# Low parts of ff1 weight chunks made by an accumulating DMA instead of a vector subtraction, and one low part of the first activations issued earlier

## The chip, the core and the metric

The kernel runs on one core of a Trainium2 chip. Its engines are TensorE (PE, with its weight loads PEld), VectorE (DVE), ScalarE (ACT), GpSimd (POOL) and SyncE (SP), which work side by side and wait for one another by semaphores. Sixteen DMA engines move data between HBM and the on-chip memory SBUF. The metric is the device time of one execution in microseconds (us); lower is better.

## The reference

One decoder layer over 256 positions of width 1024: two attention mixers side by side, their merge, and then the feed-forward part, which is all that the change touches. In the reference it is

```
h2 = rmsnorm(x, norm2_g[layer])
u = jax.nn.relu(h2 @ w_ff1[layer])          # w_ff1: 1024 x 4096
x = x + (u * u) @ w_ff2[layer]              # w_ff2: 4096 x 1024
return rmsnorm(x, norm_f_g)
```

Everything is float32.

## The kernel before

**Split products.** TensorE multiplies in a rounded format (float32r). To keep float32 accuracy each operand is split into a high part (the value rounded) and a low part (what the rounding left out), and each product is three matmuls: high times high, high times low, low times high (`mm3`, line 219). So every weight that is loaded must be split before use: `split` (line 103) lets ScalarE write the high part `whi` (line 112, a copy that rounds) and VectorE the low part `wlo = raw - whi` (line 114).

**Chunks and slots.** The weights come in chunks of 128 x 2048 float32 (1 MB), listed in `CHUNKS` (line 23) and loaded from HBM by SP's queue (`load`, line 98) into three rotating buffers `raw`. `whi` and `wlo` have three rotating buffers each too. The kernel's loop handles one chunk per slot: slot c runs the matmuls of chunk c. The feed-forward part starts at c = 28 (`C_FF`): chunk 28 is ff1 number 0, then ff1 and ff2 chunks alternate: odd c from 29 to 49 are ff1 numbers 1 to 11, even c from 30 to 50 are ff2 numbers 0 to 10. From 51 to 54 come ff1 12 to 15, from 55 to 59 ff2 11 to 15.

**An ff1 slot** is 48 matmuls of 256 columns (`wstat`, lines 239 to 247). Of each three, in the order in which the trace shows them, the third is the one that reads `wlo`. **An ff2 slot** of numbers 0 to 10 uses a scheme of seven products instead of eight (`seven_mms`, line 869): 21 matmuls of 512 columns. It needs sums of the chunk's blocks (`w_sums`, lines 838 to 845, VectorE), a split of the sums (`w_parts`, lines 855 to 862: ScalarE, then VectorE), and a split of the single blocks (`w_singles`, lines 847 to 853: ScalarE `sh`, VectorE `sl`). It also needs the activations of the ff1 slot two slots earlier: `squares` (lines 802 to 805, ScalarE), `act_sums` (line 813, VectorE) and `act_parts` (lines 820 and 822: ScalarE `ah`, VectorE `al`).

**The order.** Each engine executes its instructions in the order in which the program issues them. That order is written by hand: `at(pos, f, ...)` puts a call at the fraction pos of a slot's matmuls, and `run_slot` (line 202) issues the calls between the matmuls, sorted by position; calls of one position stand in the order in which they were put. `slot_events(c)` (line 920) prepares chunk c + 2 (and c + 3 for ff2), and issues the load of chunk c + 5, which must wait until the `raw` buffer of chunk c + 2 has had its last reader. `squares_events(i)` (line 947) is run in the slot behind ff1 number i. In slot 29 there are also the transposes of the residual into four output banks (`x1_rows`, line 754, copied out by ScalarE at line 761), the same banks in which slot 30 starts its products. In slot 32, `rstd2` (line 825) puts two squares on ScalarE.

Of the kernel before, what the change touches and what calls it, by code (L numbers as in the profile page):

```python
# [9 lines left out]
F32R = mybir.dt.float32r  # L10
AF = mybir.ActivationFunctionType
ALU = mybir.AluOpType
# [10 lines left out]
CHUNKS = (  # L23
    [("kva", i, 1536) for i in range(2)]
    + [("kvb", i, 1632) for i in range(2)]
    + [(s, i, 2048) for s in ("q", "qm", "km", "vm") for i in range(2)]
    + [("gm", i, 2048) for i in range(8)]
    + [("upn", i, 2048) for i in range(2)]
    + [("upm", i, 2048) for i in range(2)]
    + [("wout", i, 2048) for i in range(4)]  # L30
    + [("ff1", 0, 2048)]
# [4 lines left out]
NCH = len(CHUNKS)  # L36
# [9 lines left out]
def hybrid_layer(ctx: ExitStack, tc: tile.TileContext, gxd, w, w1c, small, const, gf, out):  # L46
    nc = tc.nc
    act, dve, pool, pe = nc.scalar, nc.vector, nc.gpsimd, nc.tensor
    PS = bass.MemoryType.PSUM

    wp = ctx.enter_context(tc.tile_pool(name="wp", bufs=3))
# [36 lines left out]
    raw, hi, lo = {}, {}, {}  # L88
# [110 lines left out]
    def at(pos, f, *a):  # L199
        ev.append((pos, f, a))  # L200
# [333 lines left out]
    for sec, c0, n in groups:  # L534
# [6 lines left out]
        for i in range(2):  # L541
            c = c0 + i
# [86 lines left out]
    for g in range(4):  # L629
        accs = [acc_tile(), acc_tile()]  # L630
        for i in range(2):
            c = C_GM + 2 * g + i
# [40 lines left out]
    for sec, c0, kind, evac in (("upn", C_UPN, "n", upn_evac), ("upm", C_UPM, "m", upm_evac)):  # L673
        for i in range(2):
            c = c0 + i
# [26 lines left out]
    def two_blocks(c, ah, al, late=8, whole=None):  # L702

        if late < 8:
            outs = [acc_tile()[:, 0:256] for _ in range(2)]
            whole = None
            order = [range(late), range(late, 8)]
        else:
            whole = whole or acc_tile()
            outs = [whole[:, 0:256], whole[:, 256:512]]  # L710
            order = [range(8)]
        mms = []
        for ks in order:
            for m in range(2):
                mms += wstat(outs[m], c, m * 128, 8, 256, ah, al, ks=ks, last=7)
        return mms, outs, whole
# [46 lines left out]
    for i in range(4):  # L763
        c = C_WOUT + i
# [20 lines left out]
        else:  # L785
            mms, outs, _ = two_blocks(c, mxh, mxl, 4 if i == 0 else 8)
# [48 lines left out]
    def seven(c):  # L835
        return c < NCH and CHUNKS[c][0] == "ff2" and CHUNKS[c][1] < NSEVEN
# [71 lines left out]
    def ff2_mms(i, c, p):  # L908
# [8 lines left out]
                     k == 1 and i == (13 if p == order[3] else 15))  # L917
        return r

    def slot_events(c):  # L920

        ff1 = CHUNKS[c][0] == "ff1"
        for d in (2, 3):
            if seven(c + d):
                first = c + d == C_FF + 2
                if d == 3 and not first:
                    at(0.5, w_singles, c + d, "h")
                    at(0.55, w_sums, c + d)
                elif d == 2 and first:
                    at(0.3, w_singles, c + d, "h")  # L930
                    at(0.5, w_sums, c + d)
                    at(0.55, w_parts, c + d, "h")
                    at(0.6, w_singles, c + d, "l")
                    at(0.75, w_parts, c + d, "l")
                    at(0.8, load, c + 5)
                elif d == 2:
                    at(0.05, w_singles, c + d, "l")
                    at(0.3, w_parts, c + d, "h")
                    at(0.5, w_parts, c + d, "l")
                    at(0.55, load, c + 5)  # L940
        if c + 2 < NCH and not seven(c + 2):
            for k in range(2):
                at(0.3 * k, split, c + 2, k, 2, "h")
            at(0.46, split, c + 2, 0, 1, "l")
            at(0.51, load, c + 5)

    def squares_events(i, outs, whole):
        at(0.02, squares, i, outs, whole)
        at(0.25, act_sums, i)
        at(0.4, act_parts, i, "h")  # L950
        at(0.6, act_parts, i, "l")

    fst, x1, scr = None, None, None
    for c in range(C_FF, NCH - 2):
        sec, i, _ = CHUNKS[c]
        if c == C_FF:
            lo_late(0.03, c - 1)
        slot_events(c)
        for f, a in prev:
            if f is wout_evac:  # L960
# [4 lines left out]
        if sec == "ff1":  # L965
# [13 lines left out]
            if i == NSEVEN + 1:  # L979
                at(0.1, combine, 0)  # L980
                at(0.35, combine, 1)
                at(0.7, combine, 2)
            run_slot(mms)
            prev = [(squares_events, (i, outs, whole))]
        elif i < NSEVEN:
            if i == 0:
# [147 lines left out]
```

## Time and profile before

| | |
|---|---|
| median of 3 runs | 391.09 us (390.72 to 391.92) |
| the profiled execution: its own time | 391.41 us |
| the profiled execution: span of the trace | 389.5 us |
| feed-forward slots 28 to 59 | from about 200 us to the end |

How to read what follows: the page of the profile gives for each engine its busy time, and a map of the span in 40 slices of about 9.7 us, each digit the busy share in tenths. "PEclk" is the clock that TensorE was granted, in tenths of full speed. A timeline row has the start, the duration, the engine, the line of the kernel, the instruction, what it writes and reads, and how many were merged into the row; in brackets stands idle time just before it and who ended it. A matmul's duration includes its passage through the array, so rows of back-to-back matmuls overlap: the distance from start to start is what one costs.

### The profile page before, as it was taken

What the parts mean: (1) busy time and instruction counts of PE and PEld (TensorE: products, weight loads), DVE (VectorE), ACT (ScalarE), POOL (GpSimd) and SP (SyncE); (2) the same over time, 40 slices, a digit from 0 to 9 for tenths busy, and PEclk for the clock granted to TensorE, in tenths of its full rate; (3) what the DMA queues carried; (4) which work ended last, traced back from release to release, by engine and by line L of the source; (5) the groups of instructions that cost most, each with busy time, mean ns of one, the idle gap of its engine ahead of it and who ended that gap; (6) DMA issues with size and microseconds to landing.
All of it is one profiled execution on the core that took longest, in us unless ns stands there. A gap on an engine that the chain in (4) does not pass through costs nothing.

```text
span 389.5 us, 5979 instructions
## 1 busy us (share of the span) xinstructions
PE 373.1 (96%) x2407; PEld 324.4 (83%) x2407; DVE 305.5 (78%) x443; ACT 231.4 (59%) x368; POOL 3.8 (1%) x14
## 2 busy tenths in 40 slices
PE   7999999999999999999998799999999999889993
PEld 6997888878888788779998599999998888888783
DVE  4968677887876869666969968999999999922565
ACT  6884455766755747444457567776666668451712
POOL 1000000000000000000000000000000000000001
PEclk9999999999999999999999699999999999999998
DMA  7977435233533334530846633566655556554003
GB/s 248 406 264 270 165 106 203 108 115 118 202 109 109 134 151 151 213 108 18 316 155 218 215 108 121 204 217 215 217 193 186 174 207 217 213 178 146 0 2 109
DMA packets 11260, 66.31 MB, mean 170 GB/s; under 512 B 1248, under 2 KB 2784, under 8 KB 3936
## 3 DMA queue, kind: packets, MB, share of 16 engines
q1 hardware_dynamic: 10800, 65.14, 46.8%
q10 hardware_dynamic: 432, 0.79, 0.5%
q8 instruction: 19, 0.31, 0.3%
q14 instruction: 9, 0.07, 0.0%
HBM read 64.87 MB, written 1.05 MB: 169 GB/s over the span
## 4 chain that ended last, share of the span: by engine, by line
PE 82%; DVE 8%; ACT 4%; issue 2%; DMA 1%; SPq 1%; POOLq 0%; POOL 0%; DVEq 0%; ACTq 0%
PE acc L217 51%; PE o L217 11%; PE yb L217 5%; PE tp L217 4%; DVE wlo L114 3%; PE kvbacc L217 2%; ACT whi L112 2%; PE qacc L217 2%; PE Sa L217 1%; DMA raw<-in_kva_dram 1%; PE Sb L217 1%; PE Sa L482 1%; PE Sb L482 1%; PE tp L298 1%; DVE wlo L862 1%
## 5 line engine op out<-in xcount | busy, mean ns | idle before, releaser
L114 DVE TENSOR_TENSOR wlo<-raw,whi 128x1024 fp32r<-128x1024 f32 (+3 forms) x87 | 114.5, 1333 | 28.9 <-ACT whi L112 28.8
L112 ACT ACTIVATE whi<-raw 128x1024 fp32r<-128x1024 f32 (+2 forms) x106 | 99.7, 975 | 46.9 <-PE acc L217 33.3
L217 PE MATMUL acc<-h2h,whi 128*128 128x256 f32 x240 | 66.8, 278 | 3.0 <-ACT ur L804 3.0
L217 PE MATMUL acc<-h2h,wlo 128*128 128x256 f32 x240 | 66.5, 277 | 0.0
L217 PE MATMUL acc<-h2l,whi 128*128 128x256 f32 x240 | 66.5, 277 | 0.0
L217 PE MATMUL acc<-whi,hTh 128*128 128x512 f32 (+1 forms) x128 | 50.8, 397 | 0.8 <-ACT whi L112 0.6
L217 PE MATMUL acc<-wlo,hTh 128*128 128x512 f32 (+1 forms) x128 | 50.6, 395 | 0.4 <-DVE wlo L114 0.2
L217 PE MATMUL acc<-whi,hTl 128*128 128x512 f32 (+1 forms) x128 | 49.4, 386 | 0.0
L217 PEld LDWEIGHTS acc<-h2h,whi 128*128 128x128 f32 x240 | 45.1, 188 | 3.9 <-ACT ur L804 3.4
L217 PEld LDWEIGHTS acc<-h2l,whi 128*128 128x128 f32 x240 | 45.1, 188 | 0.5
L217 PEld LDWEIGHTS acc<-h2h,wlo 128*128 128x128 f32 x240 | 45.1, 188 | 0.0
L860 ACT ACTIVATE whi<-wt 128x2048 fp32r<-128x2048 f32 x11 | 21.1, 1920 | 24.7 <-DVE wt L845 24.7
L217 PEld LDWEIGHTS acc<-whi,hTh 128*128 128x128 f32 x128 | 24.2, 189 | 6.8 <-ACT whi L112 1.1
L217 PEld LDWEIGHTS acc<-wlo,hTh 128*128 128x128 f32 x128 | 24.1, 188 | 5.5 <-DVE wlo L114 1.6
L217 PEld LDWEIGHTS acc<-whi,hTl 128*128 128x128 f32 x128 | 24.1, 188 | 4.3
L862 DVE TENSOR_TENSOR wlo<-wt,whi 128x2048 fp32r<-128x2048 f32 x11 | 25.1, 2286 | 0.4 <-ACT whi L860 0.4
L820 ACT ACTIVATE ah<-aq 128x896 fp32r<-128x896 f32 (+1 forms) x16 | 13.6, 852 | 18.1 <-PE o L217 10.0
L822 DVE TENSOR_TENSOR al<-aq,ah 128x896 fp32r<-128x896 f32 (+1 forms) x16 | 15.4, 960 | 6.7 <-ACT ah L820 6.7
L853 DVE TENSOR_TENSOR sl<-raw,sh 128x1536 fp32r<-128x1536 f32 x11 | 19.3, 1752 | 0.0
L217 PE MATMUL o<-wlo,ah 128*128 128x512 f32 (+1 forms) x47 | 18.9, 402 | 0.0
L217 PE MATMUL o<-whi,al 128*128 128x512 f32 (+1 forms) x47 | 18.8, 400 | 0.0
L217 PE MATMUL o<-whi,ah 128*128 128x512 f32 (+1 forms) x47 | 18.8, 400 | 0.0
(280 smaller groups left out, 759.5 us busy)
## 6 DMA issues: line engine op xcount, KB each, us to landing
raw<-in_ff_dram SPq DMA_DIRECT2D x32, 1024.0 KB, 4.8
raw<-in_gm_dram SPq DMA_DIRECT2D x8, 1024.0 KB, 4.8
raw<-in_wout_dram SPq DMA_DIRECT2D x4, 1024.0 KB, 4.8
raw<-in_q_dram SPq DMA_DIRECT2D x2, 1024.0 KB, 5.5
raw<-in_qm_dram SPq DMA_DIRECT2D x2, 1024.0 KB, 7.6
raw<-in_km_dram SPq DMA_DIRECT2D x2, 1024.0 KB, 5.8
raw<-in_vm_dram SPq DMA_DIRECT2D x2, 1024.0 KB, 4.8
raw<-in_upn_dram SPq DMA_DIRECT2D x2, 1024.0 KB, 4.8
```

The source lines that it names most:

```text
L112: act.activation(hi[c][:, a:b], raw[c][:, a:b], AF.Copy)
L114: dve.tensor_tensor(lo[c][:, a:b], raw[c][:, a:b], hi[c][:, a:b].bitcast(F32), op=ALU.subtract)
L217: pe.matmul(o, l, r, start=start, stop=stop, skip_group_check=True)
L298: pe.transpose(tp[:, j * 256 + t * 128:j * 256 + t * 128 + 128], src[:, t, (2 * i + j) * 128:(2 * i + j + 1) * 128], ident)
L482: pe.transpose(S[x][:, j, c:c + 128], P[:, 2 * x + j, c:c + 128], ident)
L820: act.activation(A[i][1][:, 0:b - a], aq[:, a:b], AF.Copy)
L822: dve.tensor_tensor(A[i][2][:, 0:b - a], aq[:, a:b], A[i][1][:, 0:b - a].bitcast(F32), op=ALU.subtract)
L853: dve.tensor_tensor(singles[c][1], v, singles[c][0].bitcast(F32), op=ALU.subtract)
L860: act.activation(hi[c], v, AF.Copy)
L862: dve.tensor_tensor(lo[c], v, hi[c].bitcast(F32), op=ALU.subtract)
```

## The change

Two edits. First, a new function `lo_by_dma` makes the low part of some ff1 chunks. ScalarE writes `lo = -raw`, rounded to float32r, which is the negated high part; then a DMA issued from POOL's queue reads the same chunk's raw weights from HBM once more and adds them onto `lo` in SBUF, so that `lo` becomes raw minus rounded raw. The high part is then written by one ScalarE copy of 128 x 2048 in place of two of 128 x 1024, and VectorE's subtraction of line 114 is not issued for these chunks. This holds in the slots c where chunk c + 1 is an ff2 chunk of the seven-product kind and chunk c + 2 is not: c = 29, 31, ..., 49, so for the chunks 31, 33, ..., 51 (ff1 numbers 2 to 12, eleven by this condition). `lo_by_dma` stands at the start of slot c, the high part at 0.3, the next load at 0.51. Second, for ff1 number 0 alone `act_parts(0, "l")` stands at 0.42 of slot 29 instead of 0.6.

```
+    def lo_by_dma(c):
+
+        sec, j, _ = CHUNKS[c]
+        hi[c] = wp.tile([128, 2048], F32R, name="whi")
+        lo[c] = wp.tile([128, 2048], F32R, name="wlo")
+        act.activation(lo[c], raw[c], AF.Copy, scale=-1.0)
+        pool.dma_start(out=lo[c], in_=w[sec][j], accum_op=ALU.add)
+
...
-        if c + 2 < NCH and not seven(c + 2):
+        if c + 2 < NCH and not seven(c + 2) and seven(c + 1):
+            at(0.0, lo_by_dma, c + 2)
+            at(0.3, split, c + 2, 0, 1, "h")
+            at(0.51, load, c + 5)
+        elif c + 2 < NCH and not seven(c + 2):
             for k in range(2):
                 at(0.3 * k, split, c + 2, k, 2, "h")
             at(0.46, split, c + 2, 0, 1, "l")
...
         at(0.4, act_parts, i, "h")
-        at(0.6, act_parts, i, "l")
+        at(0.6 if i else 0.42, act_parts, i, "l")
```

## The prediction

> **What bounds the kernel now.** I read the map of slices first. TensorE stands at nine tenths nearly everywhere, so it is the bound on the whole; the exceptions matter.
>
> ```profile
> span 389.5 us, 5979 instructions
> PE   7999999999999999999998799999999999889993
> DVE  4968677887876869666969968999999999922565
> PEclk9999999999999999999999699999999999999998
> ```
>
> Two things stand out. In slices 22 and 23 (214 to 234 us, the first feed-forward slots) TensorE drops to 8 and 7 and its clock to 6. And from slice 25 to 34 (244 to 341 us) VectorE too is at nine. Which of the two binds there I read from the chain of work that ended last, which shows where each ff1 slot (48 matmuls) starts:
>
> ```profile
> 224.83 5.45 PE acc L217 x48
> ...
> 286.79 5.47 PE acc L217 x48
> ...
> 329.19 5.37 PE acc L217 x47
> ```
>
> 224.83 is slot 31, 286.79 slot 43, 329.19 slot 51. Six pairs of slots (one ff1, one ff2) take 61.96 us, 10.33 each; the last four take 42.40, 10.60 each. VectorE's work in this stretch, grouped by shape:
>
> ```profile
> L114 DVE TENSOR_TENSOR wlo<-raw,whi 128x2048 fp32r<-128x2048 f32 x11 | 25.2, 2287 | 5.8 <-ACT whi L112 5.8
> L862 DVE TENSOR_TENSOR wlo<-wt,whi 128x2048 fp32r<-128x2048 f32 x9 | 20.6, 2285 | 0.0
> ...
> 260.80 2.29 DVE L114 TENSOR_TENSOR wlo<-raw,whi 128x2048 fp32r<-128x2048 f32 x1
> ...
> 271.40 2.28 DVE L114 TENSOR_TENSOR wlo<-raw,whi 128x2048 fp32r<-128x2048 f32 x1
> ```
>
> The last two rows, from VectorE's timeline, are the same subtraction in two neighbouring pairs: 10.60 apart. So VectorE needs 10.60 us per pair without a pause, TensorE 10.33. VectorE falls 0.27 behind per pair from the moment it has no pause, eats up its lead in six pairs, and is the bound in the last four.
>
> **The start** I read from the waits of TensorE and the rows of slots 29 and 30:
>
> ```profile
> PE o L217 <- DVE al L822: 2.2, 1, 2.2
> PE o L217 <- ACT x L761: 1.9, 1, 1.9
> ...
> 206.46 1.92 ACT L860 ACTIVATE whi<-wt 128x2048 fp32r<-128x2048 f32 x1 [4.12 <-DVE wt L845]
> 208.28 1.04 ACT L112 ACTIVATE whi<-raw 128x1024 fp32r<-128x1024 f32 x1
> 209.23 0.64 ACT L802 ACTIVATE ur<-acc 128x256 f32<-128x256 f32 x2
> 209.90 0.64 ACT L805 ACTIVATE aq<-ur 128x512 f32<-128x512 f32 x1
> 210.44 1.05 ACT L112 ACTIVATE whi<-raw 128x1024 fp32r<-128x1024 f32 x1
> 211.74 0.95 ACT L820 ACTIVATE ah<-aq 128x896 fp32r<-128x896 f32 x1 [0.26 <-DVE aq L813]
> 212.60 1.47 ACT L851 ACTIVATE sh<-raw 128x1536 fp32r<-128x1536 f32 x1
> 213.97 2.04 ACT L761 ACTIVATE x<-o 128x512 f32<-128x512 f32 x4
> ...
> 211.56 2.28 DVE L114 TENSOR_TENSOR wlo<-raw,whi 128x2048 fp32r<-128x2048 f32 x1
> ...
> 216.35 1.08 DVE L822 TENSOR_TENSOR al<-aq,ah 128x896 fp32r<-128x896 f32 x1
> ...
> 212.42 0.28 PE L217 MATMUL acc<-h2h,wlo 128*128 128x256 f32 x1
> 214.60 0.50 PE L217 MATMUL o<-sh,ah 128*128 128x512 f32 x1 [1.90 <-ACT x L761]
> 214.93 0.40 PE L217 MATMUL o<-sl,ah 128*128 128x512 f32 x1
> 217.49 0.79 PE L217 MATMUL o<-sh,al 128*128 128x512 f32 x1 [2.16 <-DVE al L822]
> ```
>
> Slot 29 ends at 212.7. Slot 30 waits first for ScalarE to empty its output bank, runs two matmuls, and then waits for `al`, which on VectorE stands behind the subtraction for chunk 31 and the sums for chunk 32, although its input `ah` was ready at 212.69. TensorE idles about 4.1 us, and pays again, for the clock falls:
>
> ```profile
> 216.00:217.00 1.00, 0.00 (x0) 0.00 (x0) 1.00 (x2) 0.97 (x3) 0.00 (x0) 0.77 0.89 352
> ...
> 223.00:224.00 1.00, 1.00 (x5) 0.77 (x5) 0.24 (x1) 0.00 (x0) 0.00 (x0) 0.82 0.24 98
> ```
>
> In these windows the third number from the end is the granted clock: 0.77 of a microsecond that mixes full and half speed puts the fall at 216.5, 0.82 puts the return at 223.4. From 217.49 to 223.4 TensorE works 5.9 us at half speed, which loses 2.95.
>
> **The change, part by part.** *Pairs.* VectorE loses one row of 2.287 us per pair: 10.60 - 2.29 = 8.31, below TensorE's 10.33. The four slow pairs become TensorE-bound: 4 x 0.27 = **1.1 us gained**. ScalarE must now carry it:
>
> ```profile
> L860 ACT ACTIVATE whi<-wt 128x2048 fp32r<-128x2048 f32 x9 | 17.3, 1923 | 20.6 <-DVE wt L845 20.6
> L851 ACT ACTIVATE sh<-raw 128x1536 fp32r<-128x1536 f32 x9 | 13.2, 1472 | 0.0
> L820 ACT ACTIVATE ah<-aq 128x896 fp32r<-128x896 f32 x9 | 8.6, 957 | 6.7 <-DVE aq L813 6.7
> L805 ACT ACTIVATE aq<-ur 128x512 f32<-128x512 f32 x10 | 6.3, 633 | 0.3
> L804 ACT ACTIVATE ur<-acc 128x512 f32<-128x512 f32 x10 | 5.8, 577 | 2.1 <-PE acc L217 2.1
> ```
>
> Per pair: three 128x2048 copies (negated low, high, sums) at 1.92, and 1.47, 0.96, 0.63, 0.58: 9.4 us of 10.33. In order from a pair's start: the two new copies and `sh` end near 5.2, before the accumulator that `ur` waits for is complete (5.47); `ur`, `aq`, `whi`, `ah` end near 9.6. It fits, with 0.7 to spare, so I cost it at nothing; were each copy 0.25 longer, it would bind.
>
> *The accumulating DMA* is what the trace does not show. It can start only when ScalarE has written `-raw` into a `wlo` buffer, and that buffer (one of three) is released when TensorE ends slot c - 1. So: start of slot c, plus 1.92, plus the latency L from there to landing, must not pass the third matmul of slot c + 2, two matmuls (0.23) behind that slot's start. The pair's period becomes the larger of 10.33 and 1.92 + L - 0.23 = L + 1.7; up to L = 8.6 it is hidden. Rows near to L:
>
> ```profile
> raw<-in_ff_dram SPq DMA_DIRECT2D x32, 1024.0 KB, 4.8
> 379.68 0.56 POOL L1023 TENSOR_TENSOR fst<-fst,mhalf 128x1 f32<-128x1 f32 x1 [358.47 <-DVE fst L1019]
> 259.00:260.00 1.00, 1.00 (x11) 1.00 (x11) 1.00 (x2) 1.00 (x2) 0.00 (x0) 1.00 1.02 418
> ```
>
> A plain 1 MB load lands 4.8 after its issue, while the engines, all busy (1.02), move 418 GB/s, so 2.5 of the 4.8 is moving. An estimate of POOL's part is the 0.56 of its smallest late operation. Low end: 4.8 + 0.56 = 5.4, the addition free. It reads SBUF besides HBM: a second 2.5 makes 7.9. The load of chunk c + 5 now starts when the high part is written, 3.8 into the pair, instead of after the subtraction, and shares the engines: another 2.5 makes 10.4. I take **7.9**, the middle, since the accumulation has a lead of 1.9 us over that load: hidden in an ordinary pair. It isn't hidden behind `rstd2`:
>
> ```profile
> 235.35 1.04 ACT L828 ACTIVATE fscr<-x 128x1024 f32<-128x1024 f32 x1
> ...
> 236.51 1.06 ACT L828 ACTIVATE fscr<-x 128x1024 f32<-128x1024 f32 x1
> ```
>
> These two, 2.2 us with their readouts, stand ahead of the negated copy for chunk 35 and push it some 1.5 past the start of slot 33: budget 8.6 - 1.5 = 7.1, **0.8 lost** once (0 to 3.3 between the ends). POOL's queue is otherwise empty until 379, and SP's issues move earlier; nothing else waits behind them. From slot 51 on only the starting time changes.
>
> The Trainium skill, in Collectives: The Full Stack, section The bandwidth ceiling, says that an adding DMA is slower than a copy not by the addition but by two source reads on one read ring, 32.35 against 62.28 GB/s. By that the moving would be 1.93 x 2.5 = 4.8, an estimate that speaks against the low end and for 7.7 to 10.2; no row here shows it.
>
> *The start.* ScalarE's row at 208.28 becomes a 1.92 copy. By the starts of the rows: the negated copy 208.28, `ur` 210.10 (1.82 on, as 206.46 to 208.28), `aq` 210.77, the high part 211.31, `ah` 213.13, `sh` 213.99, the bank copies 215.36; the first matmul follows 0.63 behind, as now: 215.99. `al`, now ahead of the sums and with no subtraction before it, is done at 215.2. The third matmul comes at 216.5 instead of 217.49: **1.0 gained**; ScalarE's bank copies are late next. The gap from 212.7 to 216.0 is one piece of 3.3. Clock: none of the 2.95 comes back if the half speed lasts as long, all if the fall doesn't come. I take **1.0**, nearer to the low end, for a gap remains.
>
> By the Trainium skill (TensorE: Matmul & The Clock Gate, Part 1) the gate judges fixed windows of about 3.4 us; the stretch 216.5 to 223.4 is two of them, so the trace agrees. By that rule one slow window would go and 1.2 come back instead of 1.0.
>
> Sum: 391.41 - 1.1 + 0.8 - 1.0 - 1.0 = 389.1. The profiled execution lies 0.32 above the median of the runs, so **388.8 us**.
>
> **Rivals.** *The accumulation comes late* and takes VectorE's place as the bound. Place: the third matmul of each odd slot from 33 to 51, waiting for `wlo` from a DMA. For it: two reads and a shared load give 10.4; against it: the DMA engines are free for some 40% of a pair (they show 0.54 busy in the ten-us windows). Price: ten pairs of L + 1.7. Before they took 104.36; the start gives 2.0, so it decides at 106.4, L = 8.9. At L = 10.4 the ten take 121: 391.41 + 16.6 - 2.0 - 0.32 = 405.7; at 9.6, 397.7.
>
> ```profile
> 265.00:275.00 10.00, 10.00 (x69) 9.13 (x68) 9.93 (x11) 7.26 (x7) 0.00 (x0) 1.00 0.54 201
> ```
>
> *The start gives nothing*: one more ScalarE slip (its chain has no slack there) or a slow stretch as long and later. Then only the pairs count: 388.8 + 2.0 = 390.8.
>
> **Chances.** The forecast, L at most 8.6: 0.53, its own range 386.0 to 389.8 (low end: L free, full clock). Late accumulation: 0.34, of which 0.05 within 0.3% of before, the rest slower. No gain at the start: 0.13, of which 0.10 within 0.3%. So faster 0.56, same 0.15, slower 0.29; 0.3% is 1.2 us, about what a measurement of this kernel can tell from no change. The range runs from 386.3 to 402 (L near 9.9), leaving out an estimated 0.05 below and 0.13 above.
>
> **What would show it.** Right: odd slots 10.33 apart to slot 51; VectorE at eight tenths; no wait of TensorE for a DMA but a short one in slot 35; slot 30's first matmul near 216.0 with no second gap. Wrong: `PE acc` waiting for DMA `wlo`; DMA slices at nine; raw loads landing later than 4.8; ScalarE's `ur` late, with TensorE waiting for it.

## The result

The changed kernel takes 397.04 us (median; 395.72 to 397.22) against 391.20 before: a ratio of 1.0136, 95% interval 1.0105 to 1.0168. It is slower, and the prediction said faster. Measured once more on another occasion (below) it took 398.31, a ratio of 1.0168 [1.0116, 1.0220]. Now and then an execution is slow as a whole, whatever the kernel (one of four here took 747.97 us); such ones are left out of every time and view below.

The page of the changed kernel, map of slices and DMA issues (the last column is the median time from issue to landing):

```profile
PE   7999999999999999999996999999998989889993
DVE  2959678896876868676977977678887763932464
DMA  7976535333533444521838799999999998554003
...
raw<-in_ff_dram SPq DMA_DIRECT2D x32, 1024.0 KB, 8.1
wlo<-in_ff_dram POOLq DMA_DIRECT2D x11, 1024.0 KB, 9.3
```

VectorE came down from nine tenths to mostly seven and eight, as meant. The DMA engines went up to nine from slice 23 to 32, a raw load lands after 8.1 instead of 4.8, and the adding DMA lands 9.3 after its issue. The two new or longer ones of TensorE's waits behind 196 us (in all, times, longest):

```profile
PE acc L217 <- DMA wlo<-in_ff_dram: 4.6, 6, 1.3
PE o L217 <- ACT x L761: 3.2, 1, 3.2
```

The first is new; the second was 1.9 before. One turn of the first, from the timelines of ScalarE, POOL and TensorE:

```profile
235.76 1.91 ACT L925 ACTIVATE wlo<-raw 128x2048 fp32r<-128x2048 f32 x1
...
237.96 0.86 POOL L926 DMA_DIRECT2D wlo<-in_ff_dram  x1 [10.84 <-DVE wt L842]
...
245.72 0.28 PE L217 MATMUL acc<-h2h,whi 128*128 128x256 f32 x1
245.84 0.28 PE L217 MATMUL acc<-h2l,whi 128*128 128x256 f32 x1
247.15 0.39 PE L217 MATMUL acc<-h2h,wlo 128*128 128x256 f32 x1 [1.04 <-DMA wlo<-in_ff_dram]
```

ScalarE ends the negated copy at 237.67, POOL issues 0.3 later, and TensorE, two matmuls into slot 35, stands until 247.15, 9.2 after the issue. How far the slots spread, from the first matmuls of slots 31 and 51:

```profile
224.05 0.28 PE L217 MATMUL acc<-h2h,whi 128*128 128x256 f32 x1
...
334.35 0.28 PE L217 MATMUL acc<-h2h,whi 128*128 128x256 f32 x1
```

Ten pairs took 110.30 (11.03 each) where they took 104.35. At TensorE's own 10.33 they would have taken 103.3. Of the 7.0 beyond that, the gaps before the matmuls that read `wlo`, measured from start to start and with the one step behind each, make 6.7; the clock stayed at full speed. So nearly the whole loss in the pairs is that one wait. The profiled executions differ by 5.6 in span, and it adds up from four places. Against before, the pairs lost 5.95. Before the feed-forward part the new execution was already 1.61 late; this is the same instruction of slot 27 in both, first of before, then of after:

```profile
200.45 0.51 ACT L742 ACTIVATE h2h<-gx 128x256 fp32r<-128x256 f32 x1 [2.21 <-DVE gx L739]
```

```profile
202.06 0.51 ACT L742 ACTIVATE h2h<-gx 128x256 fp32r<-128x256 f32 x1 [2.21 <-DVE gx L739]
```

From there to slot 31 it gained 2.2 (21.99 instead of 24.22), and behind slot 51 it lost 0.3. The gain is the start of slot 30:

```profile
215.66 1.09 DVE L822 TENSOR_TENSOR al<-aq,ah 128x896 fp32r<-128x896 f32 x1 [1.62 <-ACT ah L820]
...
216.91 2.04 ACT L761 ACTIVATE x<-o 128x512 f32<-128x512 f32 x4
...
217.54 0.50 PE L217 MATMUL o<-sh,ah 128*128 128x512 f32 x1 [3.23 <-ACT x L761]
...
218.10 0.46 PE L217 MATMUL o<-sh,al 128*128 128x512 f32 x1
...
218.00:219.00 1.00, 1.00 (x5) 0.79 (x4) 0.97 (x2) 1.00 (x3) 0.00 (x0) 0.65 0.87 213
...
221.00:222.00 1.00, 1.00 (x5) 0.78 (x4) 0.96 (x6) 0.90 (x1) 0.00 (x0) 0.65 0.93 393
```

One gap instead of two, ended by ScalarE's bank copies, with `al` done 0.8 before it ended. The clock fell at 218.3 and was back at 221.7: 3.4 us at half speed instead of 5.9 of matmuls.

### The profile page after: what moved, and what is told of

Its sections match the earlier page's. It is cut to its first block, busy times and chain, and to the rows that moved or that the text cites. A ratio compares the mean times of both kernels' runs of the same rounds, so it can differ in the third digit from the quotient of the medians.

```text
span 395.1 us, 5995 instructions
## 1 busy us (share of the span) xinstructions
PE 374.8 (95%) x2407; PEld 327.3 (83%) x2407; DVE 283.8 (72%) x432; ACT 249.7 (63%) x368; POOL 13.5 (3%) x25
## 3 DMA queue, kind: packets, MB, share of 16 engines
q0 software_dynamic: 1584, 11.54, 15.7%
## 4 chain that ended last, share of the span: by engine, by line
PE 58%; issue 27%; DMA 4%; ACT 4%; DVE 4%; POOL 2%; SPq 1%; POOLq 0%; DVEq 0%; ACTq 0%
PE acc L217 37%; PE yb L217 4%; PE o L217 4%; PE qacc L217 3%; PE tp L217 3%; DMA wlo<-in_ff_dram 2%; PE kvbacc L217 2%; DVE wlo L114 2%; POOL wlo L926 2%; DMA raw<-in_kva_dram 2%; ACT whi L112 1%; PE Sa L217 1%; PE Sb L217 1%; PE Sa L482 1%; PE Sb L482 1%
## 5 line engine op out<-in xcount | busy, mean ns | idle before, releaser
L112 ACT ACTIVATE whi<-raw 128x1024 fp32r<-128x1024 f32 (+3 forms) x95 | 98.7, 1066 | 46.8 <-PE acc L217 36.9
L114 DVE TENSOR_TENSOR wlo<-raw,whi 128x1024 fp32r<-128x1024 f32 (+3 forms) x76 | 89.3, 1194 | 33.2 <-ACT whi L112 33.1
L217 PE MATMUL acc<-h2h,wlo 128*128 128x256 f32 x240 | 67.6, 282 | 4.6 <-DMA wlo<-in_ff_dram 4.6
L217 PE MATMUL acc<-whi,hTh 128*128 128x512 f32 (+1 forms) x128 | 51.7, 404 | 1.1 <-ACT whi L112 1.0
L217 PE MATMUL acc<-wlo,hTh 128*128 128x512 f32 (+1 forms) x128 | 51.5, 402 | 0.3 <-DVE wlo L114 0.2
L217 PE MATMUL acc<-whi,hTl 128*128 128x512 f32 (+1 forms) x128 | 50.3, 393 | 0.0
L217 PEld LDWEIGHTS acc<-wlo,hTh 128*128 128x128 f32 x128 | 24.9, 194 | 4.7 <-DVE wlo L114 0.8
L217 PEld LDWEIGHTS acc<-whi,hTl 128*128 128x128 f32 x128 | 24.9, 195 | 4.3
L925 ACT ACTIVATE wlo<-raw 128x2048 fp32r<-128x2048 f32 x11 | 21.1, 1915 | 6.8 <-PE tp L217 6.8
L926 POOL DMA_DIRECT2D wlo<-in_ff_dram x11 | 9.7, 882 | 292.7 <-ACT wlo L925 281.9
```

Of the source, the lines that this page charges most:

```text
L112: act.activation(hi[c][:, a:b], raw[c][:, a:b], AF.Copy)
L114: dve.tensor_tensor(lo[c][:, a:b], raw[c][:, a:b], hi[c][:, a:b].bitcast(F32), op=ALU.subtract)
L217: pe.matmul(o, l, r, start=start, stop=stop, skip_group_check=True)
L925: act.activation(lo[c], raw[c], AF.Copy, scale=-1.0)
L926: pool.dma_start(out=lo[c], in_=w[sec][j], accum_op=ALU.add)
```

## The experiments

**Is it the addition, or the road through POOL?** Three theories for the landing of 9.3: the addition itself is dear (A), POOL's queue is slow (B), or the raw loads beside it take the engines (the reason for the high end of the range). First the addition was left out in place, so the low parts hold raw weights:

```
-        pool.dma_start(out=lo[c], in_=w[sec][j], accum_op=ALU.add)
+        pool.dma_start(out=lo[c], in_=w[sec][j])
```

> The changed kernel with the addition left out: POOL's DMA copies the raw weights plainly into wlo, so the low parts hold the wrong numbers; queue, size, place and waits are the same. Theory A (an adding DMA occupies the DMA engines about twice as long as a copy, because it reads two sources): landing falls from 9.3 to about 6 to 7 us after issue, busy share of the DMA engines over slots 31 to 50 from 0.95 to about 0.78, odd slots 10.33 apart, no wait of TensorE for wlo, time about 390. Rival B (the cost is POOL's issue path or sharing with the raw loads, not the addition): landing stays at 8.5 or more, odd slots 10.8 or more apart, time 395 or more.

389.01 us, 0.9934 [0.9908, 0.9960]. DMA issues, then two rows of the chain:

```profile
raw<-in_ff_dram SPq DMA_DIRECT2D x32, 1024.0 KB, 6.7
wlo<-in_ff_dram POOLq DMA_DIRECT2D x11, 1024.0 KB, 5.1
...
222.90 5.48 PE acc L217 x48
...
326.17 5.37 PE acc L217 x47
```

103.27 for ten pairs: 10.33 to the end, with the same instructions on VectorE, ScalarE, POOL's queue and SP's. The landing falls by 4.2 and every wait for `wlo` is gone. Of the 4.2, 0.3 is POOL's own issue, 0.53 for the plain transfer and 0.86 for the adding one. So it is the addition (A), and B is out; by what means the addition costs this, two reads or another, no run here separates. Queue rows of the two kernels (packets, MB, share of 16 engines), first the changed one, then the plain one:

```profile
q0 software_dynamic: 1584, 11.54, 15.7%
```

```profile
q0 software_dynamic: 1584, 11.54, 8.6%
```

15.7% of 395.1 over eleven transfers is 5.6 us of all engines for 1 MB added; 8.6% of 386.6 is 3.0 for 1 MB copied.

**Alone.** In the kernel before, behind the last load, POOL clears a free buffer, sends one adding DMA of 1 MB and, when that has landed, a plain one:

```
+    def alone():
+        z = wp.tile([128, 2048], F32R, name="wlo")
+        pool.memset(z.bitcast(F32), 0.0)
+        pool.dma_start(out=z, in_=w["ff2"][0], accum_op=ALU.add)
+        pool.dma_start(out=z, in_=w["ff2"][0])
+    at(0.0, alone)
```

> The kernel before, and in the last slot, when no load is left, POOL clears a free wlo buffer, sends one adding DMA of 1 MB onto it and then, when that has landed, a plain one of the same size; their result is not used. Theory A: the adding one lands about 7.5 to 8.5 us after issue, the plain one 2 to 3 us sooner, about 5 to 6. Rival B: both land within 1 us of each other. Opening: if a queue of POOL's DMAs in the program is what delays the first 22 us (rstd on POOL at 22.1 in the changed kernel, 20.2 before), rstd comes at about 22 here too; if that is chance, at about 20.2.

Its views: POOL's timeline, the landing of line 1048 (adding) and of line 1049 (plain), a window in the adding one (last columns: clock, share of the DMA engines, GB/s), and a row of SP's queue:

```profile
373.06 1.06 POOL L1048 DMA_DIRECT2D wlo<-in_ff_dram  x1 [0.32 <-POOL wlo L1047]
...
DMA to landing us min/median/max: 9.0/9.0/9.0
...
DMA to landing us min/median/max: 6.0/6.0/6.0
...
377.00:378.00 1.00, 1.00 (x6) 0.79 (x5) 0.97 (x2) 0.46 (x1) 0.00 (x0) 1.00 1.11 229
...
383.99 5.80 SPq L1031 DMA_DIRECT2D out_dram<-gx  x4
```

With nothing beside it the adding DMA lands after 9.0, half a microsecond past the end of what I had expected here. So the sharing with the raw loads, on which I had let the high end rest, isn't what made L long. The plain one, issued at 382.33, was not alone: the first stores of the output start at 383.99, before it lands. Its 6.0 is therefore no price of a plain transfer by itself, and the 3.0 between the two isn't one of the addition; the price comes from the version before, in place. With all engines busy the adding DMA gets 229 GB/s through, where a plain load from SP's queue got 418 in the kernel before (the window 259 to 260 of the prediction). This is one execution of 394.64 us; the two transfers hold up POOL's last operations and with them the output, so the time itself says nothing.

**Where is the limit, latency or full engines?** In place the engines are 0.95 busy, so a second limit could stand right behind the first. The changed kernel, from 224 to 327:

```profile
224.00:327.00 103.00, 98.42 (x649) 88.59 (x649) 78.78 (x94) 86.57 (x69) 8.64 (x10) 1.00 0.95 281
```

Three versions put the matmuls that read `wlo` later. In the first, all sixteen of a slot stand last:

```
+                    mms = [m for j, m in enumerate(mms) if j % 3 < 2] + mms[2::3]
```

> The changed kernel, but in the ff1 slots of numbers 2 to 12 the sixteen matmuls that read wlo stand last, so each low part is needed 3.6 us later. If only the latency of the adding DMA is the bound (it may now be 12.2 us): odd slots 10.33 apart, no wait for wlo, time about 390. If the DMA engines are full (theory A: two loads of 2.56 and about 5.4 for the adding DMA are 10.5 us of engine time per pair): odd slots 10.5 to 10.7 apart, raw loads landing late and VectorE or ScalarE waiting for raw, time 391.5 to 394.

388.75 us, 0.9903 [0.9864, 0.9941]; no trace of it is used. Both halves of a bank are open at once here, each begun by a first matmul of its own, and the sums that come out are not those of the kernel; the count and the shapes of the matmuls are the same. In the second the eight of each half stand last in their half:

> The changed kernel, but in each block of 24 matmuls of the ff1 slots of numbers 2 to 12 the eight that read wlo stand last, so a low part may land 1.8 us later (L up to 10.4). If only the latency is the bound: odd slots 10.33 to 10.4 apart, waits for wlo under 1 us in all, time about 389. If full DMA engines are the bound: odd slots 10.5 or more apart, waits for raw, 391 or more.

392.72 us, 1.0030 [0.9998, 1.0061]. The landing grew as it was given time, and waits remained:

```profile
wlo<-in_ff_dram POOLq DMA_DIRECT2D x11, 1024.0 KB, 10.4
...
PE acc L217 <- DMA wlo<-in_ff_dram: 3.7, 5, 1.8
DVE wt L842 <- DMA raw<-in_ff_dram: 9.1, 8, 2.1
```

The time, the waits for raw loads and the mean pair of 10.70 are those of the second expectation, full engines. But four of the ten pairs stand at 10.33, and what TensorE itself waits for is still `wlo`, so this version doesn't decide it.

The third is the first with only one first matmul for both halves of the bank:

> The changed kernel with the sixteen matmuls that read wlo last in the ff1 slots of numbers 2 to 12 and one start of the bank for both of its halves, so a landing up to 12.2 us is in time. Latency alone: odd slots 10.33 apart, time about 389. Engines full (their busy share was 0.95 to 0.97 in the changed kernel and in the version with 1.8 us more time): landing grows past 10.4, raw loads are waited for, odd slots 10.5 to 10.8 apart, 390.5 to 393.

389.44 us, 0.9966 [0.9941, 0.9990].

```profile
wlo<-in_ff_dram POOLq DMA_DIRECT2D x11, 1024.0 KB, 10.8
...
DVE wt L843 <- DMA raw<-in_ff_dram: 12.0, 8, 2.3
...
224.00:327.00 103.00, 102.76 (x682) 93.23 (x681) 78.66 (x95) 89.88 (x75) 8.65 (x10) 1.00 0.98 291
```

The landing is now 10.8, VectorE waits 12 us for raw loads, the DMA engines are 0.98 busy, and still eight of ten pairs stand at 10.33 (10.92 and 10.62 the others) since nobody needs the low part before 12.2. So what made the changed kernel slow was the latency against its deadline. The engines are close to being the next bound: in these three versions the landing is longer where they are fuller, though no run shows that the one makes the other.

**Fewer bytes.** Half the columns by the adding DMA, half by VectorE:

```
-        act.activation(lo[c], raw[c], AF.Copy, scale=-1.0)
-        pool.dma_start(out=lo[c], in_=w[sec][j], accum_op=ALU.add)
+        act.activation(lo[c][:, 1024:], raw[c][:, 1024:], AF.Copy, scale=-1.0)
+        pool.dma_start(out=lo[c][:, 1024:], in_=w[sec][j, :, 1024:], accum_op=ALU.add)
...
+            at(0.46, split, c + 2, 0, 2, "l")
```

> Both edits, but only columns 1024 to 2047 of each such chunk get their low part by the adding DMA (512 KB, negated copy 0.96 us); VectorE subtracts the first half (1.22 us). Theory A (the price of the adding DMA is the bytes that it adds): landing about 6.3 after issue, VectorE 9.5 per pair, busy share of the DMA engines about 0.75, odd slots 10.33 apart, no wait for wlo, and the bank copies at the start about 0.9 us earlier than in the changed kernel: time 387.5 to 388.5. Rival (a fixed latency of POOL's adding DMA, whatever its size): landing 8.6 or more, odd slots 10.5 or more apart, 390.5 or more.

387.80 us, 0.9913 [0.9887, 0.9939], faster than before and than the change:

```profile
wlo<-in_ff_dram POOLq DMA_DIRECT2D x11, 512.0 KB, 6.7
...
222.77 5.47 PE acc L217 x48
...
315.71 5.37 PE acc L217 x47
...
224.00:327.00 103.00, 103.00 (x690) 93.89 (x689) 90.73 (x105) 81.32 (x74) 8.60 (x10) 1.00 0.82 248
```

Nine pairs in 92.94, 10.33 each; VectorE is busy 9.1 per pair, inside TensorE's pace, and TensorE waits for no low part.

**The two edits apart.** The second alone, on the kernel before:

> The second edit alone on the kernel before (al of ff1 number 0 at 0.42). If the wait for al at the start is worth what the trace of before shows: third matmul of slot 30 near 215.2 instead of 217.5, VectorE's chain about 2.3 us earlier from there on and still 10.60 per pair at the end, time about 389. Rival (VectorE must idle a microsecond for ah in slot 29, and as the bound of the later pairs it gives the gain back): 390.5 to 391.5.

389.24 us, 0.9945 [0.9919, 0.9972]. TensorE's start of slot 30 and a window over the pairs:

```profile
214.07 0.50 PE L217 MATMUL o<-sh,ah 128*128 128x512 f32 x1 [1.89 <-ACT x L761]
...
214.64 0.39 PE L217 MATMUL o<-sh,al 128*128 128x512 f32 x1
...
244.00:327.00 83.00, 83.00 (x542) 73.97 (x541) 81.56 (x82) 58.26 (x58) 0.00 (x0) 1.00 0.56 200
```

The second gap is gone, 3.5 gained from slot 27 to slot 31 (20.67 instead of 24.22); then VectorE, 81.56 of 83 us busy, holds eight of the ten pairs at 10.53 to 10.64 and takes 0.9 of it back. The first edit alone:

> The first edit alone (al of ff1 number 0 back at 0.6). If in the changed kernel the start hangs on ScalarE's bank copies and no longer on al: al would be done near 217.7 on the changed kernel's clock, before the third matmul there (218.1), so the second edit is worth nothing beside the first and the time is that of the changed kernel within 1 us, 396.5 to 398.5. Rival (the second edit carries the whole gain at the start): 2 us more, 399 or above, with TensorE waiting for al.

397.43 us, 1.0180 [1.0133, 1.0227]. Its row of slot 27, and its third matmul of slot 30, which finds `al` done at 216.85:

```profile
201.28 0.51 ACT L742 ACTIVATE h2h<-gx 128x256 fp32r<-128x256 f32 x1 [1.93 <-DVE gx L739]
...
217.50 0.63 PE L217 MATMUL o<-sh,al 128*128 128x512 f32 x1
```

From slot 27 to slot 31 it takes 21.99, as the changed kernel does. The changed kernel again:

> The changed kernel once more, for its spread and its opening. Odd slots about 11.06 apart again and landing about 9.3 whatever the opening does. If the 1.9 us by which rstd on POOL came later in its first profile is chance, rstd is nearer to 20.2 to 20.9 here, as in the other kernels, and the time 395.5 to 396.5; if it belongs to the change, rstd is at 22 and the time 397 again.

398.31 us, with ten pairs in 111.39. The two agree within their spread: beside the first edit the second is worth nothing that shows, since the subtraction that stood before `al` is gone anyway.

**On from the better version.** The bank copies ahead of the singles copy, in the half version, in the second edit alone, and with a quarter of the columns added:

```
-                at(0.5, lambda: x1_rows(range(4), [o_bank(k) for k in range(4)]))
+                at(0.49, lambda: x1_rows(range(4), [o_bank(k) for k in range(4)]))
```

> As the half version, and the transposes of the residual with their four bank copies on ScalarE stand ahead of the singles copy for chunk 32 in slot 29 (0.49 instead of behind it at 0.5). If ScalarE's bank copies are what the start of slot 30 waits for: its first matmul about 1.4 us earlier than in the half version, perhaps without a fall of the clock, time 385.5 to 387. If another wait takes its place (al, or sh behind the bank copies): within 0.5 us of the half version.

387.42 us, 0.9893 [0.9849, 0.9936]. Start, clock, and what came of it:

```profile
214.09 0.50 PE L217 MATMUL o<-sh,ah 128*128 128x512 f32 x1 [1.00 <-ACT x L761]
...
217.00:218.00 1.00, 1.00 (x6) 0.82 (x5) 0.97 (x2) 0.97 (x2) 0.00 (x0) 1.00 0.56 139
...
DMA to landing us min/median/max: 5.4/6.3/8.2
...
274.79 0.38 PE L217 MATMUL acc<-h2h,wlo 128*128 128x256 f32 x1 [0.87 <-DMA wlo<-in_ff_dram]
```

The idle time is down to 1.0 and the clock doesn't fall: slot 31 comes 2.7 sooner than in the half version (18.43 behind the row of slot 27 instead of 21.15). But two pairs of 11.5 give 2.4 back, most of it in two waits for `wlo`. For slot 41 the transfer was issued at 266.51 and landed late, after 8.2; for slot 35 the negated copy stood behind the two squares of `rstd2`, and the transfer was issued only at 235.76, 6.2 into slot 33.

> The second edit alone with the bank copies ahead of the singles copy, no adding DMA. If VectorE is the bound of everything behind the start (10.60 per pair): slot 30 begins 1.4 us earlier, but the odd slots fall back to VectorE's pace and the time stays within 0.7 of the second edit alone, 388.5 to 389.5. Rival (TensorE is the bound): 1.4 us less, about 387.8 or below.

389.54 us, 0.9964 [0.9947, 0.9981]: nothing over the second edit alone. Slot 31 comes 2.8 sooner (17.91 behind the row of slot 27), but VectorE is the bound: nine of the ten pairs stand 10.6 apart. The other one took 12.69: there VectorE, which has no lead left, waits 1.5 for ScalarE behind the squares of `rstd2`.

> As the half version with the bank copies ahead, but the adding DMA makes only columns 1536 to 2047 (256 KB); VectorE subtracts 1536 columns (1.75 us), 10.03 per pair. Theory A: landing about 5 us, no wait for wlo anywhere (the half version had two, 1.5 us), odd slots 10.33 apart, time 385.8 to 387. Rival (VectorE with 0.3 to spare falls behind through its own waits): odd slots 10.4 to 10.6 apart, 387.5 to 389.

387.20 us, 0.9901 [0.9878, 0.9924]; no trace of it is used, so that it lost the two waits isn't shown. The three versions at 387.2 to 387.8 can't be told apart.

## Why the prediction was wrong

**The pairs' bound, and VectorE's relief: right.** With the addition left out the pairs stand at 10.33 to the end, on the same engines' work.

**ScalarE fits: right.** In the same run it is busy 9.0 of each 10.33, where the rows added up to 9.4, and holds nothing up.

**The start: right in size and mechanism.** 2.0 forecast, 2.2 found. There is one gap, ended by the bank copies. The third matmul of slot 30, less the 1.61 by which this execution was late, stands at 216.49 for the 216.5 forecast. Of the half-speed loss 1.25 came back (2.95 less half of 3.4), where I took 1.0; the Trainium skill's window rule (TensorE: Matmul & The Clock Gate, Part 1), one window of about 3.4 us in place of two, gave 1.2, and the trace agrees. What the prediction didn't see is that the second edit adds nothing to it here: the first, which takes the subtraction from before `al`, brings the same 21.99 alone.

**The adding DMA: here the prediction failed**, in the step "I take 7.9, the middle". The mechanism stood there as the first rival, with its place, and even with its price for L = 9.6: 397.7. L was 0.3 from ScalarE's end to POOL's issue plus 9.3, so 9.6. The plain road was priced about right, 5.4 for 5.1. Two terms were too small: the hand-off of 0.3 was left out, and the addition, priced at 2.5 as a second read at the rate of a plain load, costs 4.2 in place, 0.3 of it POOL's longer issue. My reason for the middle, that a lead of 1.9 over the next load spares it the sharing, looked at the wrong thing: alone it lands after 9.0 already, past the 8.6 (less the hand-off, 8.3) that a pair has. The Trainium skill's ratio (Collectives: The Full Stack, The bandwidth ceiling), 1.93 between two collectives, one that adds and one that copies, is near that of the engine time here: 5.6 over 3.0 is 1.87.

**The term behind `rstd2`: right in place.** The negated copy for chunk 35 starts 1.4 past slot 33, for the 1.5 forecast, and slot 35 waits; the pair behind it takes 11.64, 1.3 lost instead of 0.8, since L was longer.

**The period L + 1.7: too simple.** It gives 11.3, and 11.03 was found. Single pairs go from 10.33 to 11.88. The wait lies inside a slot, behind the release of the buffer for the next negated copy, so a slot that waits gives the next low part more time; this is read from the rows and wasn't tried. So it is in part luck that the rival's 397.7 lies so near the 397.04: it has 2.7 too much in the ten pairs, and nothing for the 1.6 of the opening. (The upper end of the range, 402, is by the prediction's own sum an L of 10.0, not 9.9.)

**Left open.** The 1.61 of the opening, the stretch before the feed-forward part, for which the prediction had no term. In it `rstd` on POOL comes at 22.1 instead of 20.2. In profiles without a POOL DMA it came at 20.2, 20.2 and 21.0, in those with one at 20.4 to 22.1, and in the changed kernel's second profile at 21.1. Chance and the mere presence of that queue aren't told apart.

## What to carry to other kernels

Work moved from a busy engine to a transfer is paid in latency against the reuse of its buffer, not in busy share: before making such a move, measure that transfer alone at its size, and compare it with the deadline set by buffer release on one side and first use on the other, with room to spare, since in place it can land later (here 9.3 to 10.8 for 9.0). If it misses by one or two microseconds, move the first use back or move only as much of the work as the engine is over its budget: here half of it was enough. And an edit that opens a start gains only until the next bound takes it back; name that bound first.

## What the runs showed of the hardware that I had not expected

An adding DMA of 1 MB, issued from POOL, got 197 to 229 GB/s through while the engines were 0.95 to 1.11 busy, where a plain load from SP's queue got 418 at 1.02; in place it holds the engines 5.6 us, a plain one on the same queue 3.0. The landing of a transfer that shares the engines is no constant of its size: its median was 9.3, 10.4 and 10.8 for the same 1 MB in versions whose engines were 0.95, 0.97 and 0.98 busy. But share alone doesn't set it: the traced execution of the first edit alone, a long one of 400.67 us, had 9.5 at 0.92.
